# A hybrid decoder trunk: a new order of the RWKV-7 recurrence's steps, two buffers for b and the scaled k, and every level of the triangular inverse crossing array rows

## The chip, the cores and the metric

The kernel runs on one core of one Trainium2 chip. The metric is the device time of one execution in microseconds (us). Timed runs are given as the median of three. A profile is one further execution with its own time; spans in the trace are measured from its first to its last instruction.

## The reference, cut to what matters

Two layers over 256 tokens of width 1024. Layer 0 mixes with a short gated convolution, layer 1 with RWKV-7 time mixing; each is wrapped in two half-step SwiGLU networks (width 2816). All of it is float32. The part that the change touches is the time mixing of layer 1, 16 heads of 64:

```python
def step(S, inp):
    r_t, w_t, k_t, v_t, a_t, b_t = inp
    sa = jnp.einsum('bhij,bhj->bhi', S, a_t)
    S = S * w_t[:, :, None, :] + sa[..., None] * b_t[:, :, None, :] + v_t[..., None] * k_t[:, :, None, :]
    y = jnp.einsum('bhij,bhj->bhi', S, r_t)
    return S, y
...
y = wkv7_scan(rh, decay, kh, vh, -kk, kk * ah)      # kk: k scaled by k_k, normalised per head
y = group_norm(y) * ln_w + ln_b + sum(r * k * r_k) * v
out = (y * g) @ w_o
```

S is a 64x64 state per head. The kernel does not step through tokens one by one: it takes chunks of 64 tokens, in which the recurrence becomes a few 64x64 products and the inverse of a unit lower triangular 64x64 matrix.

## The kernel before, in words

The wide products (the four SwiGLU networks, the convolution's projections) run as three float32r products each (high x high, high x low, low x high); weights are loaded raw, split into a high and a low part by ScalarE (ACT) and VectorE (DVE), and multiplied on TensorE (PE). They take the span up to about 640 us and from about 910 us on.

Between lies the recurrence (`rwkv_heads`). It has eight units: unit n is a group q = n // 2 of four heads and a half t = n % 2 of the 256 tokens, that is 128 tokens or two chunks (c = 0, 1) of 64. Four heads sit as two pairs (q or p in the code) of two (e = 0, 1), and e picks the upper or lower 64 partitions. Each unit goes through four generators, which are advanced step by step:

- `front(n)`, letter F, 19 steps, F0 to F18. F0: matmul `z` (decay and gate adapters). F1: POOL `kk`, ACT tanh `sa`. F2: ACT square of `kk` into `b` (a scratch use of the buffer), DVE `am` twice. F3: matmul `cum`. F4: DVE sum `ss`, POOL power `rn`. F5: DVE `PP`, ACT exponentials `P`, `PP`. F6: POOL `rt`, DVE `kk`. F7: DVE `b`, `PP`. F8: ACT exponential `iP`, DVE `b`, `iP` (the scaled k), POOL `am`. F9, F11: PE transposes `wT`; F10, F12: ACT copies `ar`, `bk`. F13: matmuls `G`. F14: DVE predicated copy into `xfix`, then the first `pb` of the inverse. F15: DVE `br`. F16, F17: DVE `ar`, and four loads each that copy `b` and `iP` by DMA into `bkt`. F18: PE transpose `PT`, ACT `pc`, DVE `bon`.
- `inverse(n)`, letter I, 12 steps (L508 to L540). Even steps I0, I2, ... I10 are the matmuls of levels 1, 2, 4, 8, 16, 32 (eight of 64x64 stationary, 128 moving columns, 64 at level 32; a float32 matmul is two instructions in the trace, so 16). Odd steps make the next level's operands: DVE transposes `pb` out of PSUM (L512) and masks it (L514), ACT copies `xr` out of PSUM (L508); before level 32 DVE makes `p` (L519) instead. I5 and I7 also issue the loads of `hvu`, the v of chunk 0 and 1.
- `chain(n)`, letter C, 12 steps, six per chunk (`wkv_chunk`). C0: matmuls `ch<-hvu,ar`. C1: ACT copy `rc`. C2: matmuls with `tt`. C3: copies `hvu` (DVE, ACT) and `y` (ACT). C4: matmuls with `bkt` and `br`. C5: DVE `hvu` of the next chunk, DVE `y`.
- `finish(n)`, letter N, 8 steps: group norm of y on DVE, ACT and POOL, matmul `g` (N3), DVE (N4, N5), PE transposes `oT` (N6), split (N7).

A score, one string per row, gives the order in which all of this is issued. Row n (n = -2 to 7) holds front(n+2), inverse(n+1), chain(n) and finish(n-1), up to front steps that are ahead or behind. Below, "I2 of unit 3" and the like name a step and its unit. The star is a filler: half of a projection or output product, six float32r matmuls of 256 columns or three of 512 (`pj`), which need no result of the units under way. L calls `feed`, which issues the loads of filler weights (`hl_n`, 512 KB) into eight buffers, and from the 72nd filler on also the first weights of the last network (`w0h` to `w1l`); k and w load rows of vectors. The order of the score is the program order of PE, ACT and DVE, which is kept; all these loads go through SP's one queue. A last string, `end`, orders what follows row 7: the finish of unit 7, the last fillers and the first products of the last network.

In the inverse, `src` is a pair of PSUM banks, one per chunk c. A matmul of half e reads the 64 array rows of e (SBUF partitions) and writes the 64 columns `to` (PSUM partitions). At levels 1 and 32 `to` is e; at levels 2 to 16 chunk 1 writes to the other half. Buffers of the pools are released to the next writer when the last reader is done; `b` and `iP` have one buffer each.

Of the kernel before, what the change touches and what calls it, by code (L numbers as in the profile page):

```python
# [18 lines left out]
F = 2816  # L19
# [6 lines left out]
class Trunk:  # L26
# [463 lines left out]
    def wkv_inverse(self, pool, u, par, duo):  # L490

        nc = self.nc
        x1, p32 = self.xfix[par], self.p32[par]
        all4 = lambda m: m.unsqueeze(1).broadcast_to([128, 4, 64])
        by2 = lambda z: z.rearrange("p (c q) m -> p c q m", c=2)
        src = duo.rearrange("p c (q i m) -> p c q i m", q=2, i=2)

        def ready(l):  # L500

            old = by2(x1[:, :, 1]) if l == 1 else src[:, :, :, 1]
            xr = pool.tile([128, 4, 2, 64], F32, name=f"xr{par}", bufs=1) if l > 1 else x1

            def rest():
                if l > 1:
                    n = 2 if l < 32 else 1
                    nc.scalar.copy(xr.rearrange("p (c q) i m -> p c q i m", c=2)[:, :, :, 0:n], src[:, :, :, 0:n])  # L508

            if l < 32:  # L510
                pb = pool.tile([128, 4, 64], F32, name=f"pb{par}", bufs=1)
                nc.vector.transpose(by2(pb), old)  # L512
                rest()
                nc.vector.tensor_tensor(pb, pb, all4(self.lev[l]), ALU.mult)  # L514
            else:
                pb = p32
                for e in range(2):
                    lo, hi = slice(64 * e, 64 * e + 32), slice(64 * e + 32, 64 * e + 64)
                    nc.vector.transpose(by2(pb)[hi, :, :, 0:32], old[lo, :, :, 32:64])  # L519
                rest()  # L520
            return pb, xr

        pb, xr = ready(1)
        yield
        for l in (1, 2, 4, 8, 16, 32):
            n = 2 if l < 32 else 1
            for q in range(2):
                for c in range(2):
                    for e in range(2):

                        to = e ^ (c if 1 < l < 32 else 0)
                        re, out = slice(64 * e, 64 * e + 64), slice(64 * to, 64 * to + 64)
                        i = 2 * c + q
                        self.mm(src[out, c, q, 0:n], pb[re, i], xr[re, i, 0:n])
            yield
            if l < 32:
                pb, xr = ready(2 * l)
            else:
                u["tt"] = pool.tile([128, 2, 2, 64], F32, name="tt", bufs=2)
                nc.scalar.copy(u["tt"], src[:, :, :, 0])  # L540
            yield
# [288 lines left out]
    def rwkv_heads(self, pool, prm, krv, lora, gT, g2, rows, row_tile, P, loaded, follow,  # L830
# [5 lines left out]
        T2 = lambda name, b=1: pool.tile([128, 256], F32, name=name, bufs=b)  # L836
# [5 lines left out]
        def front(n):  # L842
# [3 lines left out]
            u = dict(bon=s4("bon", 4), hvu=[])  # L846
            us.append(u)
            k, r = (krv[q, i][:, t] for i in "kr")
            P, iP, PP, kk, b, am, rt = (T2(i) for i in ("P", "iP", "PP", "kk", "b", "am", "rt"))

            sa = pool.tile([128, 2, 256], F32, name="sa")
            z = self.tr_bank("z").rearrange("p (i n) -> p i n", i=2)
# [45 lines left out]
            for pair, own in (((PP, rt), True), ((b, iP), False)):  # L898
# [6 lines left out]
                for j in range(2):  # L905
                    if own:
                        for e in range(2):
                            re = slice(64 * e, 64 * e + 64)
# [143 lines left out]
        def filler():  # L1052
# [15 lines left out]

        score = (
            'FFF',  # L1070
            '***LFFFFF****FLFFFF***FLF****LFFF***FLFF****FL',
            'I*FFILFFFII**FFLFII**FFILIFF*LkFIIF**FFLIIFFF**L',
            'I*FCFIFL*CFFICCIL*F*FICFFICFICLCFILCIFFICFF*FLIICCFFF**L',
            'I*FCFIFL**CNFFICNCINL**F*FICFFICFNICLNCFINLkCIFFINCFF**NFLIICCFFF**L',
            'I*FCFIFL*CNFFICNCINL**F*FICFFICFNICLNCFINLCIFFINCFF*NFLIICCFFF**Lw',
            'I*FCFIFL**CNFFICNCINL**F*FICFFICFNICLNCFINLkCIFFINCFF**NFLIICCFFF**L',
            'IFCFIFL*CNFFICNCINL*FFICFFICFNICLNCFINLCIFFINCFF*NFLIICCFFF*Lw',
            'I**FCFIFCLNFFICNICN**FLFF**ICICNFIFCFLCNINF**LCIFICFF**NFNLIICC**L',
            'ICI*CLICNNICN**LICICNILCCNINL*CIICN*NLIICC*Lw',
            'CCL*CNNC*NLC*C*LNCCN*NLCC*NNL*CC*L',  # L1080
        )
        fronts = (step for n in range(8) for step in front(n))
        feed()
        for _ in score[0]:
            next(fronts)
        with self.tc.manual_schedule(engines={mybir.EngineType.Activation, mybir.EngineType.DVE}):
            for n, order in zip(range(-2, 8), score[1:]):
                steps = dict(F=fronts, C=chain(n) if n >= 0 else None, N=finish(n - 1) if n >= 1 else None,
                             I=us[n + 1]["inv"] if -1 <= n < 7 else None)
# [16 lines left out]

        post = lambda: posts.popleft()()
        last = finish(7)
        end = 'NN*N**LLL**L*L*L*LLL**PNLNP01NNN2ooooP3P4567'
        for i in end:  # L1110
            if i == "N":
                next(last)
# [90 lines left out]
```

## Time and profile before

| | us |
|---|---|
| median of 3 runs | 1098.09 |
| lowest, highest | 1096.61, 1101.34 |
| the profiled execution | 1098.65 |
| its span in the trace | 1096.9 |

| engine | busy us | share of the span | instructions |
|---|---|---|---|
| PE (matmul) | 1063.9 | 97% | 6480 |
| DVE | 687.4 | 63% | 980 |
| ACT | 529.2 | 48% | 781 |
| POOL | 99.7 | 9% | 179 |

Busy time of an engine is the union of its instructions' durations. PE's matmuls overlap one another, so a busy PE need not be a PE at its peak; where small matmuls run, the distance from one start to the next tells more. The idle time before an instruction is shown in brackets with what ended it. In the windows view each row is one stretch: its length, then busy time (and number of instructions) of PE, PEld (weight loads), DVE, ACT and POOL in this order, then the granted TensorE clock as a share of full speed (1.00 is 2.4 GHz, half is 1.2 GHz), the DMA engines' busy share and the GB/s moved.

### The profile page before, as it was taken

Reading aid. Unit: us, or ns where it says so; the run is one execution under the profiler, and the core shown is the slowest. Engines: PE = TensorE matmul, PEld = TensorE weight load, DVE = VectorE, ACT = ScalarE, POOL = GpSimd, SP = SyncE. Lnnn points to the kernel's source line nnn. Section 1 sums busy time; section 2 is a strip of 40 time slices with the busy share of each in tenths; the row PEclk is TensorE's granted clock in tenths of the full one; section 3 lists DMA queues with packets and bytes.
Section 4 is the critical chain, followed back from the end, with each engine's and each line's share of the span. In section 5 each row is a group of like instructions: output and inputs, shape, how many; then the busy total and the mean of one; then the engine's idle time right before and its main releaser. Section 6 shows DMA issues by size and latency. Waiting matters only on the chain.

```text
span 1096.9 us, 16693 instructions
## 1 busy us (share of the span) xinstructions
PE 1063.9 (97%) x6480; PEld 875.9 (80%) x6480; DVE 687.4 (63%) x980; ACT 529.2 (48%) x781; POOL 99.7 (9%) x179
## 2 busy tenths in 40 slices
PE   7999999999999999999999999998998989999997
PEld 5888888788878888887888888987877768888886
DVE  5666554786666654567665546657889866555534
ACT  7555443655565554356544433434544426444342
POOL 6000000000320000000000001212423210000000
PEclk9999999999999999999999999999999999999999
DMA  8998877698699987679998854774553846666541
GB/s 287 314 294 273 292 244 258 210 360 269 202 302 345 284 285 261 210 260 309 320 295 296 295 191 138 275 231 147 163 160 119 269 133 191 190 191 208 179 170 39
DMA packets 178167, 259.39 MB, mean 236 GB/s; under 512 B 24238, under 2 KB 142758, under 8 KB 178088
## 3 DMA queue, kind: packets, MB, share of 16 engines
q1 hardware_dynamic: 178088, 258.32, 71.4%
q8 instruction: 51, 0.84, 0.3%
q14 instruction: 28, 0.23, 0.1%
HBM read 216.34 MB, written 38.80 MB: 233 GB/s over the span
## 4 chain that ended last, share of the span: by engine, by line
PE 68%; issue 18%; DVE 6%; DMA 3%; ACT 2%; SPq 2%; POOL 0%; POOLq 0%; ACTq 0%; DVEq 0%
PE gu L113 10%; PE gu L114 9%; PE gu L112 9%; PE acc L113 5%; PE acc L114 5%; PE acc L112 5%; PE pair L113 2%; PE pair L114 2%; PE pair L112 2%; PE ci L113 2%; PE ci L114 2%; PE ci L112 2%; SPq L50 2%; PE pj L112 2%; PE aT L351 1%
## 5 line engine op out<-in xcount | busy, mean ns | idle before, releaser
L107 DVE TENSOR_TENSOR lo_gu<-raw_gu,hi_gu 128x2048 fp32r<-128x2048 f32 (+2 forms) x92 | 198.5, 2160 | 109.6 <-ACT hi_gu L106 106.0
L113 PE MATMUL gu<-lo_gu,xh 128*128 128x512 f32 x640 | 252.9, 395 | 2.9 <-DVE lo_gu L107 2.9
L114 PE MATMUL gu<-hi_gu,xl 128*128 128x512 f32 x640 | 252.8, 395 | 0.0
L112 PE MATMUL gu<-hi_gu,xh 128*128 128x512 f32 x640 | 250.4, 394 | 1.0 <-ACT xh L178 1.0
L106 ACT CAST hi_gu<-raw_gu 128x2048 fp32r<-128x2048 f32 (+2 forms) x92 | 164.9, 1796 | 33.7 <-PE gu L114 11.8
L107 DVE TENSOR_TENSOR lo_o<-raw_o,hi_o 128x2048 fp32r<-128x2048 f32 x48 | 109.2, 2291 | 112.4 <-ACT hi_o L106 111.1
L113 PEld LDWEIGHTS gu<-lo_gu,xh 128*128 128x128 f32 x640 | 120.5, 188 | 28.5 <-DVE lo_gu L107 4.9
L106 ACT CAST hi_o<-raw_o 128x2048 fp32r<-128x2048 f32 x48 | 90.7, 1909 | 103.2 <-PE acc L114 68.5
L112 PEld LDWEIGHTS gu<-hi_gu,xh 128*128 128x128 f32 x640 | 120.4, 188 | 24.8 <-ACT xh L178 1.4
L114 PEld LDWEIGHTS gu<-hi_gu,xl 128*128 128x128 f32 x640 | 120.5, 188 | 23.6 <-DVE xl L180 0.4
L113 PE MATMUL acc<-lo_o,ah 128*128 128x512 f32 (+1 forms) x316 | 122.4, 387 | 1.4 <-DVE lo_o L107 1.4
L114 PE MATMUL acc<-hi_o,al 128*128 128x512 f32 (+1 forms) x316 | 122.4, 387 | 0.0
L112 PE MATMUL acc<-hi_o,ah 128*128 128x512 f32 (+1 forms) x316 | 117.4, 388 | 0.0
L345 ACT ACTIVATE s<-gu,rs 128x256 f32<-128x256 f32 x80 | 38.0, 475 | 97.2 <-PE gu L114 97.2
L150 POOL TENSOR_TENSOR rs<-ms,fixed 128x1 f32<-128x1 f32 x14 | 8.9, 638 | 817.9 <-DVE ms L148 817.7
L113 PEld LDWEIGHTS acc<-lo_o,ah 128*128 128x128 f32 x316 | 59.4, 188 | 13.6 <-DVE lo_o L107 1.8
L112 PEld LDWEIGHTS acc<-hi_o,ah 128*128 128x128 f32 x316 | 59.4, 188 | 11.9
L114 PEld LDWEIGHTS acc<-hi_o,al 128*128 128x128 f32 x316 | 59.4, 188 | 11.8
L117 ACT CAST ah<-aT 128x512 fp32r<-128x512 f32 x44 | 25.8, 586 | 82.2 <-PE aT L351 82.1
L349 DVE SCALAR_TENSOR_TENSOR a<-gu,rs,s 128x256 f32<-128x256 f32 x80 | 38.1, 481 | 35.3 <-ACT s L345 35.3
L602 ACT CAST hl_p<-hl_p 128x512 fp32r<-128x512 f32 x72 | 44.3, 624 | 28.3 <-DMA hl_p<-in_rwkv_w_rkv_dram 19.2
L603 DVE TENSOR_TENSOR hl_p<-hl_p 128x512 fp32r<-128x512 f32 x72 | 48.3, 686 | 4.0 <-ACT hl_p L602 3.7
(270 smaller groups left out, 1674.6 us busy)
## 6 DMA issues: line engine op xcount, KB each, us to landing
raw_gu<-in_ffn_w_gu_dram SPq DMA_DIRECT2D x164, 512.0 KB, 5.6
raw_o<-in_ffn_w_d_dram SPq DMA_DIRECT2D x44, 1024.0 KB, 5.9
parts<-hl_p SPq DMA_DIRECT2D x72, 512.0 KB, 7.0
hl_n<-parts SPq DMA_DIRECT2D x52, 512.0 KB, 4.6
hl_p<-in_rwkv_w_rkv_dram SPq DMA_DIRECT2D x48, 256.0 KB, 7.3
raw_ci<-in_conv_w_in_dram SPq DMA_DIRECT2D x14, 512.0 KB, 7.7
raw_ci<-in_conv_w_in_dram SPq DMA_DIRECT2D x4, 1024.0 KB, 8.1
raw_o<-in_conv_w_out_dram SPq DMA_DIRECT2D x4, 1024.0 KB, 8.8
```

Source lines behind the costliest of these rows:

```text
L50: return self.tc.keep_in_program_order(self.nc.sync.dma_start(dst, src))
L106: nc.scalar.copy(hi[:, ks], raw[:, ks])
L107: nc.vector.tensor_tensor(lo[:, ks], raw[:, ks], hi[:, ks].bitcast(F32), ALU.subtract)
L112: keep(mm(out, xh, wh, start=start, stop=False))
L113: keep(mm(out, xh, wl, start=False, stop=False))
L114: keep(mm(out, xl, wh, start=False, stop=stop))
L117: keep(self.nc.scalar.copy(hi, src))
L345: act = nc.scalar.activation(s, ps[t][:, 0:256], AF.Silu, scale=rstd[t])
L349: nc.vector.scalar_tensor_tensor(a, ps[t][:, 256:512], rstd[t], s, ALU.mult, ALU.mult)
L351: nc.tensor.transpose(out=pt[:, j, t * 128:t * 128 + 128], in_=a[:, j * 128:(j + 1) * 128], identity=self.ident)
L602: nc.scalar.copy(hi, lo)
L603: nc.vector.tensor_tensor(lo.bitcast(F32R), lo, hi.bitcast(F32), ALU.subtract)
```

## The change

Three edits. The crossing of chunk 1 to the other half of the columns is done at all six levels (the slice `out` is `e ^ c` always). `b` and `iP` get two buffers each; the other front tiles keep one. The ten rows of the score after the first, and the string `end`, are written anew with the same letters in all (96 fillers, 60 feeds, 149 F after the first three, 96 I, 96 C, 56 N); where a row's count changes, steps pass to a neighbour row. Fillers by row, from -2 to 7: before 21, 10, 7, 10, 8, 10, 4, 12, 6, 8; after 20, 11, 8, 9, 8, 8, 6, 11, 7, 8.

```diff
@@ wkv_inverse
-                        to = e ^ (c if 1 < l < 32 else 0)
-                        re, out = slice(64 * e, 64 * e + 64), slice(64 * to, 64 * to + 64)
+                        re, out = slice(64 * e, 64 * e + 64), slice(64 * (e ^ c), 64 * (e ^ c) + 64)
                         i = 2 * c + q
                         self.mm(src[out, c, q, 0:n], pb[re, i], xr[re, i, 0:n])
@@ front
-            P, iP, PP, kk, b, am, rt = (T2(i) for i in ("P", "iP", "PP", "kk", "b", "am", "rt"))
+            P, PP, kk, am, rt = (T2(i) for i in ("P", "PP", "kk", "am", "rt"))
+            iP, b = (T2(i, 2) for i in ("iP", "b"))
@@ score (rows -2 to 7)
-            '***LFFFFF****FLFFFF***FLF****LFFF***FLFF****FL',
-            'I*FFILFFFII**FFLFII**FFILIFF*LkFIIF**FFLIIFFF**L',
-            'I*FCFIFL*CFFICCIL*F*FICFFICFICLCFILCIFFICFF*FLIICCFFF**L',
-            'I*FCFIFL**CNFFICNCINL**F*FICFFICFNICLNCFINLkCIFFINCFF**NFLIICCFFF**L',
-            'I*FCFIFL*CNFFICNCINL**F*FICFFICFNICLNCFINLCIFFINCFF*NFLIICCFFF**Lw',
-            'I*FCFIFL**CNFFICNCINL**F*FICFFICFNICLNCFINLkCIFFINCFF**NFLIICCFFF**L',
-            'IFCFIFL*CNFFICNCINL*FFICFFICFNICLNCFINLCIFFINCFF*NFLIICCFFF*Lw',
-            'I**FCFIFCLNFFICNICN**FLFF**ICICNFIFCFLCNINF**LCIFICFF**NFNLIICC**L',
-            'ICI*CLICNNICN**LICICNILCCNINL*CIICN*NLIICC*Lw',
-            'CCL*CNNC*NLC*C*LNCCN*NLCC*NNL*CC*L',
+            '**F*FFFL***FFLFF*FF***FL**F*FLFF****LFF*FF*L*',
+            'FIFIF*F*IFL**IFF*FL*IILF*FIILFF*kFIIF**FLFIIFFLF*',
+            'I*FCFIFL*CFICLF*I*CFFICFFIL*CFICICFILCFI*CFFF*FLIILCCF*',
+            'FFFI*FFCLC*NFI*FCNCILIN*F*FICFFICFNICLNCFINLkCIFINCFF*F**NFLIICCFFF*L',
+            'FI*CLFIFFCNFI*CNCIN**LF*FICFFIFCNICLNCILNFCIFINFCFF**NFLIICCFFF*Lw',
+            '*IFCFI*CNFLNFFICCIN*L**FFICFFICICLFNCNLINFkCIFFINC*FF*F*NLICICFFFL',
+            '*IFFIC*LCFIFNCNC*INF*L*FFICFFICFILFNCNCNLCIIFIFCNFFF*ICCLNLwI',
+            'FFF*I*FCFIFC*LNFICNIF*CN**FLFFICICNFIFCFLNINCI*LCFFICFLF**NI*ICN*CL',
+            'FICI*CNNIC*LLICN*I*CICNILCCNINL*CIINCN*L*IICCLw',
+            'CNCL*NCC*NL*CC*LNNCNC*LCC*NNL*CC*L',
@@ end
-        end = 'NN*N**LLL**L*L*L*LLL**PNLNP01NNN2ooooP3P4567'
+        end = 'NN*N**LLL***L*L*LLLL*N*PLNPN01NN2ooooP3P4567'
```

## Rows read from the trace of the kernel before

**Rows 1.** The profile page: span, and busy time of TensorE.
```profile
span 1096.9 us, 16693 instructions
...
PE 1063.9 (97%) x6480; PEld 875.9 (80%) x6480; DVE 687.4 (63%) x980; ACT 529.2 (48%) x781; POOL 99.7 (9%) x179
```

**Rows 2.** Windows view, one row per unit, from level 1 of units 0 to 7.
```profile
723.72:741.49 17.77, 15.80 (x205) 13.48 (x205) 12.03 (x28) 7.96 (x19) 4.07 (x5) 1.00 0.70 225
741.49:761.89 20.40, 17.58 (x271) 14.44 (x271) 14.57 (x39) 9.89 (x28) 4.46 (x7) 1.00 0.50 154
761.89:782.44 20.55, 20.00 (x287) 16.85 (x286) 17.28 (x46) 10.21 (x29) 6.61 (x8) 1.00 0.53 161
782.44:802.58 20.14, 19.09 (x283) 15.85 (x282) 18.15 (x48) 10.29 (x29) 6.85 (x10) 1.00 0.45 133
802.58:823.57 20.99, 20.13 (x287) 16.88 (x287) 17.78 (x46) 10.69 (x30) 6.64 (x8) 1.00 0.62 177
823.57:842.61 19.04, 16.62 (x259) 13.02 (x258) 17.58 (x46) 9.29 (x28) 6.92 (x10) 1.00 0.28 79
842.61:863.62 21.01, 20.63 (x266) 15.34 (x265) 18.92 (x48) 9.56 (x28) 5.54 (x7) 1.00 0.75 234
863.62:880.45 16.83, 14.32 (x205) 10.05 (x205) 13.61 (x37) 5.59 (x16) 2.40 (x3) 1.00 0.88 291
880.45:896.50 16.05, 15.63 (x118) 11.16 (x119) 9.31 (x24) 3.66 (x12) 2.34 (x4) 0.89 0.15 48
```

**Rows 3.** Timeline of TensorE: start, length, instruction, [idle before it, what ended it].
```profile
782.44 1.09 PE L54 MATMUL pair<-xfix,pb 64*64 64x128 f32 x16
...
790.90 0.45 PE L54 MATMUL ch<-hvu,br 64*64 64x64 f32 x8
...
792.93 0.67 PE L54 MATMUL pair<-xr,pb 64*64 64x128 f32 x16
...
798.61 0.68 PE L54 MATMUL pair<-xr,p 64*64 64x64 f32 x16 [0.65 <-ACT xr L508]
```

**Rows 4.** Timeline of ScalarE: the two long waits of F2.
```profile
725.50 0.42 ACT L860 ACTIVATE b<-kk 128x256 f32<-128x256 f32 x1 [3.89 <-DMA bkt<-b]
...
744.06 0.42 ACT L860 ACTIVATE b<-kk 128x256 f32<-128x256 f32 x1 [3.29 <-DMA bkt<-b]
```

**Rows 5.** Timeline of TensorE: the waits that follow those two.
```profile
727.60 0.34 PE L54 MATMUL pair<-xr,pb 64*64 64x128 f32 x4 [1.45 <-ACT xr L508]
...
746.16 0.34 PE L54 MATMUL pair<-xr,pb 64*64 64x128 f32 x4 [0.72 <-ACT xr L508]
...
747.39 0.27 PE L54 MATMUL ch<-rc,tt 64*64 64x64 f32 x2 [0.57 <-ACT rc L559]
```

**Rows 6.** Timeline of SP's queue: weight loads, and the hvu loads behind them.
```profile
866.41 0.51 SPq L50 DMA_DIRECT2D hl_n<-parts  x1
...
872.55 4.36 SPq L50 DMA_DIRECT2D hvu<-pv  x4
```

**Rows 7.** Timeline of TensorE in row 7 of the score.
```profile
880.45 1.21 PE L54 MATMUL ch<-hvu,ar 128*64 128x64 f32 x16 [2.22 <-DMA hvu<-pv]
...
884.07 0.50 PE L112 MATMUL pj<-hl_n,oh 128*128 128x512 f32 x1
...
888.86 0.69 PE L54 MATMUL ch<-hvu,ar 128*64 128x64 f32 x16
...
890.74 0.50 PE L112 MATMUL pj<-hl_n,oh 128*128 128x512 f32 x1
```

**Rows 8.** Windows view of the stretch behind that wait (clock 0.63).
```profile
880.45:885.00 4.55, 4.55 (x34) 3.06 (x34) 0.28 (x1) 1.08 (x4) 0.00 (x0) 0.63 0.51 166
```

**Rows 9.** Timeline of VectorE at the start of unit 3's level 1 turnaround.
```profile
783.58 0.45 DVE L512 STREAM_TRANSPOSE pb<-pair 128x256 f32<-128x256 f32 x1 [0.40 <-PE pair L54]
...
784.91 0.42 DVE L873 TENSOR_TENSOR PP<-cum,sa 128x256 f32<-128x256 f32 x1 [0.42 <-PE cum L54]
```

**Rows 10.** Timeline of TensorE in the end string, unit 7's transposes.
```profile
902.40 0.33 PE L57 MATMUL oT<-fixed,y 128*128 128x128 f32 x1 [0.51 <-DVE y L993]
```

## The prediction

> **What bounds the kernel now.** The page comes first: TensorE is busy for 1063.9 of 1096.9 us [rows 1], so time can come only from the 33 us in which it idles or from matmuls that take longer than they need. The windows, unit by unit, say where the idle time lies. Before 640 us TensorE is dense; in the nine stretches from 723.72 to 896.50 us, which are rows -1 to 7 of the score, it idles (length less PE busy) 1.97, 2.82, 0.55, 1.05, 0.86, 2.42, 0.38, 2.51 and 0.42 us, together 13.0 us [rows 2]. The same rows give the second limit. VectorE idles only 3.27, 1.99, 3.21, 1.46 and 2.09 us in rows 1 to 5 (lengths 19.04 to 21.01), and part of this is the pause between its 46 to 48 instructions. So the full rows are bound by two engines at once: TensorE first, VectorE one to three us behind. The timelines then name the waits. Six are long enough to count alone: 1.45, 0.72 and 0.57 us [rows 5], 2.22 us [rows 7], 0.65 us at level 32 [rows 3] (such a wait stands in five units: four of 0.65, one of 0.34), 0.51 us in the end string [rows 10].
>
> **The crossing.** At level 1 the sixteen instructions take 1.09 us, at a crossed level of the same shape 0.67 us [rows 3]: the crossed four start together, the uncrossed in twos. That is 0.42 us less for level 1 in each of eight units. Level 32, uncrossed, takes 0.68 us; a crossed level with 64 columns isn't in the trace. Its bounds: nothing saved (0.68), or as many starts as the eight instructions of `ch<-hvu,br`, four pairs of 64 columns in 0.45 us [rows 3], so 0.23 saved; below nothing I see no reason, since the same four squares of the array are used at levels 2 to 16. I take 0.23, because the level with 128 columns did gain by four starts. Sum: 8 x (0.42 + 0.23) = 5.2 us, bounds 3.4 and 5.2. No instruction is added; six crossings bring chunk 1 back to its half as four did.
>
> The Trainium skill, TensorEngine Tiling (Array Packing), section Restrictions and Gotchas, says that different row tiles cannot access the same PSUM bank simultaneously. In this kernel e = 0 and e = 1 are two row tiles that write one chunk's bank, in different partitions. By that rule the two would take turns, crossed or not, and the sum of this part would be 0; the row with 0.67 us for the crossed level speaks against it.
>
> **Two buffers for b and iP.** F2 writes its square into `b` while the previous unit's `bkt` loads still read it: ScalarE waits 3.89 and 3.29 us for that DMA [rows 4]. Behind the square stand F4's sum on VectorE, then the level's transposes (VectorE takes its instructions in the written order), then ScalarE's `xr`, and TensorE waits 1.45 us in row -1, 0.72 + 0.57 us in row 0 [rows 5]. With two buffers the last reader of the buffer is a whole unit back (some 20 us), so both waits go: 2.74 us. What is late next is `cum` and the turnaround itself, which have two fillers beside them in the new rows. Later units lack the wait, since their F2 comes after the loads. Nothing is added on a queue. Bounds: 0 (another link holds level 2 as long) to 2.74; I take 2.7.
>
> **The loads of unit 7's v.** The 2.22 us wait is for `hvu` [rows 7]. Counting what each L issues: before, the fourth weight batch since row 5 (two `hl_n`, four pieces of the last network's weights, 2 MB) is issued in row 6 just ahead of I5 of unit 7, so the `hvu` loads stand behind it in SP's queue: the batch is issued from 866.41 us, `hvu` from 872.55 us, with 4.36 us for four issues [rows 6], while the DMA engines are 0.88 busy at 291 GB/s in this row [rows 2]. At that rate 2 MB are 7 us. In the new row 6 the two L stand together two fillers earlier and find no free buffer, so the batch moves to the L after I6, behind chunk 0's `hvu`. Chunk 0's loads then come at least the wait earlier: 2.22 us. Chunk 1's stand behind the batch, but are read only in the middle of row 7. The batch itself serves the end string.
>
> Right after that wait the granted clock is 0.63 over 4.55 us [rows 8], a stretch at the half level. C0, filler, C2 up to the next filler take 3.62 us there (880.45 to 884.07), and 1.88 us for the same steps of chunk 1 (888.86 to 890.74) [rows 7]: 1.74 us lost. Without the wait I expect no drop: 1.7 us. Bounds for the whole part: 0 (the loads stay late) to 3.9.
>
> **The end string.** N3 to N5 come before the first products of the last network, so N6 finds y finished: 0.5 us [rows 10], with 0 as the other bound.
>
> **The order.** Idle time left in rows 2 is 13.0 - 2.7 - 2.2 = 8.1 us: the bounds of what order alone can give are 8.1 and, since waits can also be made, some way below nothing. What I see in it: fillers go from rows that are full (row 3: 10 to 8, row 5: 12 to 11) to rows where TensorE waits (row 4: 4 to 6, where it idles 2.42 us; row -1; row 6), which costs nothing where it fills waits. F15 (`br`, a product of the kind that takes 0.42 us in rows 9) goes behind I9, so `p` for level 32 is made earlier, and the fillers before F18 are split, against the 0.65 us. In row 1 `cum` goes ahead of level 1, so VectorE has `PP` to do in place of its two waits of 0.40 and 0.42 us [rows 9]. Against it: in row 3 I6 follows I4 with only C4 and F11 between, N3 having moved behind; in row 4 I7 stands behind the four VectorE products of N4 and N5; F1 to F3 of unit 3 have one filler in place of two. I take 2.5 us won, about a third of 8.1, because the level 32 waits alone are 2.9 (four of 0.65, one of 0.34), and 2.5 us lost again: 0.5 in the places just named, and 2.0 because in rows 2, 4 and 5, where VectorE idles least, the crossing's 0.65 us each only moves TensorE into waiting.
>
> **Sum.** 5.2 + 2.7 + 2.2 + 1.7 + 0.5 + 2.5 - 2.5 = 12.3 us. All of it lies in the chain, since TensorE is dense again from the first products of the last network on. The profiled execution took 1098.65 us (span 1096.9), 0.6 above the median of the runs; 1098.65 - 12.3 = 1086.3, and from the median 1085.8. I forecast 1086.
>
> **Rivals.**
> 1. VectorE becomes the bound of rows 1 to 6. For it: idle times of 1.5 to 3.3 us there [rows 2]; against it: these are still more than the 0.65 us per row that the crossing takes. The crossing then pays only in two of the eight units and order gives nothing: 12.3 - 2.5 - 6 x 0.65 + 2.0 = 7.9, so 1090.7. Chance 0.25.
> 2. `hvu` of unit 7 is still late, behind the batch of row 5 that is issued at that row's end, and the clock falls again: 12.3 - 3.9 = 8.4, so 1090. For it: DMA busy at 0.88 in that row. Chance 0.12.
> 3. Slower: the turnaround of a level runs out of cover. Between two levels stand `pb` (a transpose of 0.45 us [rows 9] and a masking product) and `xr`; a unit has six such turns, so 48. If the new order puts one VectorE product of 0.42 us [rows 9] ahead of each and no filler beside it, 48 x 0.42 = 20 us come in, less 12.3: 1106. It decides from 12.3 / 48 = 0.26 us per turnaround on. For it: VectorE's density; against it: the new rows keep most groups of F and I as they were. Chance 0.09.
> 4. The crossing does not do what it says, because the two row tiles of one bank take turns: 12.3 - 5.2 = 7.1, so 1091.5. Levels 2 to 16 speak against it. Chance 0.03. This is where the Trainium skill's rule above would lead.
> 5. The new order makes as many waits as it takes away while one of the other parts fails: some 3.5 us won, 1095. Chance 0.10.
>
> **How the numbers follow.** The forecast has 0.41, its own range 1082 to 1089. About 0.5% (5.5 us) is what a measurement of this kernel can tell from no change; the bound is 1092.6. Faster: 0.40 of the forecast, 0.21 of rival 1, 0.10 of 2, 0.02 of 4, 0.01 of 5: 0.74. Slower, past 1103.6: rival 3, 0.08. Same: the rest, 0.18. The range is 1080 to 1096: below, order gives 6 of the 8.1 us and loses nothing; above, rivals 1, 2 and 5 are in; rival 3 is left out.
>
> **What would show it.** Level 1's sixteen matmuls in 0.67 us and level 32's in 0.45. No wait of `b` for `bkt` on ScalarE, and level 2 of unit 0 without its 1.45 us. C0 of unit 7 without a wait for `hvu`, and a granted clock of 1.00 in that stretch. TensorE idle under 9 us from level 1 of unit 0 to the end of row 7. Wrong would be: matmul starts of level 1 still in twos; VectorE idle under 1 us in rows 1 to 5 with TensorE idle as before; a new wait of over 1 us at `pair<-xr,pb` in rows 3 or 4.

## The result and the profile after

| | before | after |
|---|---|---|
| median, us | 1097.35 (1095.72 to 1101.34, 4 runs) | 1086.56 (1086.32 to 1088.63, 4 runs) |
| ratio, 95% interval | | 0.9898 [0.9879, 0.9917] |
| profiled execution, its span, us | 1098.65, 1096.9 | 1088.63, 1086.9 |

The time lies 0.6 us from the forecast, inside the range and 10.8 us under the time before. First the page of the changed kernel, beside [rows 1]: the work is the same (6480 matmul records), TensorE is busy 3.8 us less and the span is 10.0 us shorter.

```profile
span 1086.9 us, 16688 instructions
...
PE 1060.1 (98%) x6480; PEld 872.9 (80%) x6480; DVE 686.5 (63%) x980; ACT 528.8 (49%) x781; POOL 100.1 (9%) x179
```

Where it lies is told by one window over the whole recurrence, from its first matmul `z` to the first `gu` product of the last network (the products that `end` issues lie inside). Windows view; before, then after (columns as in [rows 2]):

```profile
703.97:914.61 210.64, 197.08 (x2434) 159.46 (x2432) 160.10 (x408) 95.71 (x262) 53.41 (x71) 0.99 0.56 171
```

```profile
705.65:904.60 198.95, 190.98 (x2434) 154.06 (x2432) 159.36 (x408) 95.50 (x262) 53.94 (x71) 1.00 0.59 181
```

The recurrence is 11.69 us shorter: 5.59 us of TensorE's idle time (13.56 to 7.97) and 6.10 us of its busy time. What follows takes 182.3 us in both. What comes ahead is 1.68 us longer in this execution of after (705.65 instead of 703.97): its granted clock is 0.91 over the first 20 us, where before has 1.00 and which the change does not touch, and its other three runs lie some 2 us lower. The length of the recurrence is used below for the experiments, since it leaves such things out. Windows view of after, rows -1 to 7, which answers to [rows 2]:

```profile
725.00:740.30 15.30, 15.30 (x209) 13.42 (x209) 10.32 (x24) 7.47 (x19) 3.71 (x5) 1.00 0.84 284
740.30:759.00 18.70, 17.88 (x279) 14.85 (x278) 15.24 (x40) 9.82 (x28) 4.46 (x7) 1.00 0.65 200
759.00:778.37 19.37, 18.89 (x281) 15.56 (x281) 17.79 (x46) 10.54 (x30) 6.52 (x8) 1.00 0.52 151
778.37:797.48 19.11, 18.80 (x287) 15.65 (x287) 17.83 (x48) 10.22 (x30) 7.12 (x10) 1.00 0.44 133
797.48:816.38 18.90, 18.12 (x276) 14.86 (x275) 17.17 (x44) 10.04 (x30) 6.66 (x8) 1.00 0.70 182
816.38:836.87 20.49, 17.57 (x272) 13.91 (x271) 17.93 (x47) 9.80 (x29) 7.13 (x10) 1.00 0.37 112
836.87:856.18 19.31, 19.18 (x256) 13.77 (x255) 18.49 (x47) 9.44 (x27) 5.76 (x7) 1.00 0.76 223
856.18:872.17 15.99, 14.23 (x209) 9.91 (x208) 12.92 (x37) 5.63 (x17) 2.28 (x3) 1.00 0.95 304
872.17:886.28 14.11, 14.11 (x118) 10.09 (x119) 10.02 (x26) 3.59 (x12) 2.38 (x4) 1.00 0.18 65
```

Length less PE busy is 0, 0.82, 0.48, 0.31, 0.78, 2.92, 0.13, 1.76 and 0 us, together 7.2 where 13.0 stood. Two rows keep a hole: row 4 (816.38), which had 2.42, and row 6 (856.18). The granted clock is 1.00 in every row. Timeline of TensorE of after: a last level (32) and the first level behind it, and the waits that are left:

```profile
793.40 0.41 PE L57 MATMUL PT<-fixed,P 128*128 128x128 f32 x2 [0.28 <-DVE br L930]
793.74 0.46 PE L54 MATMUL pair<-xr,p 64*64 64x64 f32 x16
...
797.48 0.67 PE L54 MATMUL pair<-xfix,pb 64*64 64x128 f32 x16
...
823.35 0.41 PE L57 MATMUL wT<-fixed,PP 128*128 128x128 f32 x2 [0.99 <-DVE PP L881]
...
832.90 0.41 PE L57 MATMUL PT<-fixed,P 128*128 128x128 f32 x2 [1.30 <-DVE br L930]
...
872.17 0.69 PE L54 MATMUL ch<-hvu,ar 128*64 128x64 f32 x16 [1.62 <-issue]
...
890.04 0.50 PE L114 MATMUL pair<-w0h,xl 128*128 128x512 f32 x1 [0.77 <-DVE xl L180]
```

### The profile page after: what moved, and what is told of

It reads as the page before. It is cut to its first block, busy times and chain, and to the rows that moved or that the text cites. A ratio compares the mean times of both kernels' runs of the same rounds, so it can differ in the third digit from the quotient of the medians.

```text
span 1086.9 us, 16688 instructions
## 1 busy us (share of the span) xinstructions
PE 1060.1 (98%) x6480; PEld 872.9 (80%) x6480; DVE 686.5 (63%) x980; ACT 528.8 (49%) x781; POOL 100.1 (9%) x179
## 4 chain that ended last, share of the span: by engine, by line
PE 73%; issue 18%; DVE 5%; ACT 1%; DMA 1%; SPq 1%; POOL 0%; POOLq 0%; DVEq 0%; ACTq 0%
PE gu L113 10%; PE gu L114 10%; PE gu L112 10%; PE acc L113 5%; PE acc L114 5%; PE acc L112 5%; PE pj L112 2%; PE pair L114 2%; PE pair L113 2%; PE pair L112 2%; PE ci L113 2%; PE ci L114 2%; PE ci L112 2%; PE pj L113 2%; PE pj L114 2%
## 5 line engine op out<-in xcount | busy, mean ns | idle before, releaser
L150 POOL TENSOR_TENSOR rs<-ms,fixed 128x1 f32<-128x1 f32 x14 | 11.2, 798 | 819.7 <-DVE ms L148 819.5
```

The costliest lines, as they stand in the source:

```text
L150: self.last_rs = nc.gpsimd.tensor_tensor(rs, ms[:, 1:2], self.nhalf[:, 0:1], ALU.pow)
```

## The experiments

Each was timed in turn with the kernel before on one chip. Before has its own column, since the groups ran on different chips, which differ by over 1 us: compare medians down the column only with that in mind. The clock is the mean granted clock of the runs (before: 0.9971, 23 runs, in the first group). The last column, the median of each run's time multiplied by its own clock, is an estimate of the time at full clock, in which all of the time is taken to follow the clock; for before it is some 1094 to 1095. The clock of a run is known to three digits (half a us), and where a part of the time does not follow the clock the estimate is too low: a straight line through the 12 runs of the crossing alone reaches 1094.1 us at clock 1.00, one through the 23 runs of before beside it 1095.2. The profile is that of one of the runs. For the crossing alone it is the longest of its 12 (1105.92 us, clock 0.986), for the kernel with levels 1 and 32 twice the shortest (1094.96 us, clock 0.999), so the lengths of these two recurrences differ by far more than their medians.

| kernel | median us (runs) | before, same chip | ratio [95%] | recurrence in the profile, us | clock | at full clock |
|---|---|---|---|---|---|---|
| before + crossing | 1100.78 (12) | 1098.19 | 1.0024 [1.0009, 1.0038] | 217.86 | 0.9914 | 1090.7 |
| before + buffers | 1096.16 (12) | 1098.19 | 0.9986 [0.9974, 0.9999] | 210.46 | 0.9972 | 1093.3 |
| before + order | 1094.30 (5) | 1098.19 | 0.9965 [0.9951, 0.9978] | 206.09 | 0.9978 | 1091.4 |
| after without crossing | 1090.31 (5) | 1098.19 | 0.9933 [0.9919, 0.9947] | 202.72 | 0.9988 | 1089.2 |
| after without buffers | 1091.22 (6) | 1096.77 | 0.9953 [0.9937, 0.9970] | 202.27 | 0.9968 | 1087.7 |
| before + early `hvu` loads | 1094.62 (12) | 1096.77 | 0.9979 [0.9967, 0.9991] | 209.26 | 0.9971 | 1091.3 |
| before + crossing + buffers | 1096.01 (12) | 1097.98 | 0.9975 [0.9957, 0.9993] | 206.91 | 0.9934 | 1088.6 |
| before + crossing, levels 1 and 32 twice | 1096.94 (12) | 1097.98 | 0.9992 [0.9978, 1.0006] | 206.60 | 0.9978 | 1094.5 |
| after | 1086.56 (4) | 1097.35 | 0.9898 [0.9879, 0.9917] | 198.95 | 0.9988 | 1085.8 |

**The crossing alone, in the old order.**

```diff
-                        to = e ^ (c if 1 < l < 32 else 0)
-                        re, out = slice(64 * e, 64 * e + 64), slice(64 * to, 64 * to + 64)
+                        re, out = slice(64 * e, 64 * e + 64), slice(64 * (e ^ c), 64 * (e ^ c) + 64)
```

> The kernel before with the crossing at levels 1 and 32 alone. Theory (the crossing is worth what its matmuls lose): level 1 goes from 1.09 to 0.67 us, level 32 from 0.68 to 0.45, 0.65 us in each of eight units, so 5.2 us less, ratio 0.9953. Rival (VectorE bounds rows 1 to 6): the same shorter levels, but TensorE waits as much longer in those rows, and 1.3 us are left, ratio 0.9988. If level 32 does not start in fours, 3.4 us.

It is slower, which was not foreseen: 2.6 us by the medians. In this profile, the longest of the 12 runs, the recurrence is 7.2 us longer than in before, with less work in it. Windows view of this kernel, the recurrence and three short stretches:

```profile
704.02:921.88 217.86, 202.41 (x2433) 163.17 (x2432) 159.22 (x408) 95.64 (x262) 53.38 (x71) 0.94 0.55 165
...
729.00:733.00 4.00, 4.00 (x33) 3.48 (x32) 2.37 (x6) 2.53 (x7) 0.72 (x1) 0.57 1.02 381
749.50:753.50 4.00, 3.97 (x28) 3.69 (x28) 2.62 (x6) 1.63 (x5) 1.75 (x5) 0.57 0.75 246
804.00:808.00 4.00, 4.00 (x22) 3.63 (x16) 2.93 (x11) 0.90 (x2) 0.00 (x1) 0.57 0.18 74
```

The clock is 0.57 in these stretches, most of each at the lower level, and as low at three more places of the recurrence; before has one such stretch [rows 8], which is also the last of these six. What TensorE did just ahead of the three shown is in its timeline:

```profile
728.14 0.67 PE L54 MATMUL pair<-xr,pb 64*64 64x128 f32 x16 [2.37 <-ACT xr L508]
...
748.29 0.67 PE L54 MATMUL pair<-xr,pb 64*64 64x128 f32 x16 [1.73 <-ACT xr L508]
...
802.58 0.46 PE L54 MATMUL pair<-xr,p 64*64 64x64 f32 x16 [0.65 <-ACT xr L508]
803.30 0.45 PE L574 MATMUL ch<-hvu,bkt 128*64 128x64 f32 x8 [0.26 <-ACT y L570]
```

The waits that were 1.45 and 0.72 us [rows 5] are 2.37 and 1.73. Some 0.4 us of each increase is the time that level 1 saves: `xr` still comes when ScalarE is through with its own wait for the DMA, so there the saved time turns into idle time. The rest is that wait itself, which in this execution was 4.39 and 3.88 us where before had 3.89 and 3.29 [rows 4]. At level 32 the saving is lost too in five of the eight units: it takes 0.46 instead of 0.68 us, but right behind it comes a new wait of 0.26 us for ScalarE's `y`, where before has none, and the next matmuls start 0.72 us after level 32 in both. Elsewhere the saving of level 1 stays: row 3, at clock 1.00, takes 20.15 us (808.13 to 828.28), and 20.58 in the next kernel, in which these levels take as long as uncrossed.

So the crossing alone does save time, but less than its 5.2 us: at full clock this kernel would stand at 1090.7 to 1094.1 us, between 1 and 4 us under before by the same two estimates. The fallen clock takes more than that back. It falls behind the two long waits and, as at 804 us, behind the short ones of level 32 (0.65 and 0.26 us), where before has 0.65 us alone and kept 1.00 in its profile.

**Is it the clock?** The same kernel with the eight matmuls of levels 1 and 32 issued twice (the second time the same values into the same place), so that each level takes as long as uncrossed (1.10 and 0.69 us in its timeline): more work, and the saved time is not idle time.

```diff
-            for q in range(2):
+            for q in (0, 1) * (2 if l in (1, 32) else 1):
```

> The crossing alone, with the matmuls of levels 1 and 32 issued twice (the second writes the same values), so that these levels take about as long as uncrossed. It has 128 matmul instructions more at level 1 and 128 more at level 32 than the crossing alone and no wait less. Theory (the clock is what the crossing alone lost): the mean granted clock comes back to about 0.997, the time to that of the kernel before or less, ratio 0.998 to 1.000, so faster than the crossing alone (1.0024) with more work. Rival (the crossed matmuls themselves cost something, such as a change of the array's rows and columns): it costs twice as often, ratio 1.005 or above.

With 256 more matmul records the median of 12 runs is 3.8 us lower than with the crossing alone, on another chip; the intervals of the two ratios do not touch. Between the two profiles, the longest run of the one and the shortest of the other, the recurrence is 11.3 us shorter. Windows view:

```profile
704.28:910.88 206.60, 195.88 (x2689) 158.79 (x2688) 159.24 (x408) 95.71 (x262) 53.42 (x71) 1.00 0.58 174
```

The clock is 1.00, and 0.9978 in the mean of the 12 runs where the crossing alone has 0.9914. Matmuls that compute nothing new make the kernel faster, so it was the shorter work, by way of the clock, that did the harm, and not the crossed matmuls, of which there are more here. At full clock this kernel is not faster than before (1094.5).

**The buffers alone.**

```diff
-            P, iP, PP, kk, b, am, rt = (T2(i) for i in ("P", "iP", "PP", "kk", "b", "am", "rt"))
+            P, PP, kk, am, rt = (T2(i) for i in ("P", "PP", "kk", "am", "rt"))
+            iP, b = (T2(i, 2) for i in ("iP", "b"))
```

> The kernel before with two buffers for b and iP alone. Theory: ScalarE's waits of 3.89 and 3.29 us for the bkt loads go, and with them TensorE's 1.45, 0.72 and 0.57 us: 2.7 us less, ratio 0.9975. Rival: another link of the chain (cum, P, the next xr) holds level 2 in rows -1 and 0 as long, and nothing is won, ratio 1.000.

Level 2 of units 0 and 1, the two places of [rows 5] (timeline of TensorE):

```profile
728.90 0.67 PE L54 MATMUL pair<-xr,pb 64*64 64x128 f32 x16 [0.31 <-ACT xr L508]
...
748.92 0.67 PE L54 MATMUL pair<-xr,pb 64*64 64x128 f32 x16 [0.31 <-ACT xr L508]
```

In this profile rows -1 and 0 take 16.59 and 18.80 us, 2.78 less than in [rows 2], against 2.7 in the forecast. The recurrence as a whole is only 0.2 us shorter in this one execution: its clock falls at two places (797.9 us, behind a wait of 0.64 us at level 32, and 879.9 us) where before's does so once, and C0 of unit 7 waits 3.08 us for `hvu` where it waited 2.22 [rows 7], so that a part of what was won is waited for there. By the medians 2.0 us are left.

**Crossing and buffers, old order.** Both edits on the kernel before.

> The kernel before with the crossing and the two buffers, old order. Theory (the crossing alone lost because TensorE then rests longer in the old order's waits and its granted clock falls to half; the buffers take the two longest of these waits away): the mean clock is nearer to that of the kernel before (0.997) than to that of the crossing alone (0.991), and the time is 3 to 5 us less than before, ratio 0.9955 to 0.997. Rival (the crossing is worth nothing in the old order, whatever the clock): as the buffers alone, ratio 0.9986 or above.

The clock comes only part of the way back, 0.9934 after 0.9914 (0.9971 before), and the ratio 0.9975 misses the range that was expected: the two waits of the buffers are not the only places where the crossing costs clock. In this profile it falls at three, behind the waits of level 32 in rows 0 and 4 and at C0 of unit 7, which waits 2.24 us for `hvu`. The place in row 0 (windows view, timeline of TensorE):

```profile
756.00:760.00 4.00, 4.00 (x24) 3.58 (x26) 2.30 (x8) 0.90 (x2) 0.51 (x1) 0.57 0.24 94
```

```profile
754.22 0.46 PE L54 MATMUL pair<-xr,p 64*64 64x64 f32 x16 [0.65 <-ACT xr L508]
```

The median is 4.8 us under that of the crossing alone, on two chips. By the two ratios the crossing is worth 1.2 us beside the buffers (0.9986 to 0.9975), and 3.5 to 4.7 at full clock.

**The order alone.** The score and the string `end` of after in the kernel before.

> The kernel before with the new score and end string alone, no crossing, one buffer each. Theory (the parts add up): the whole change is 11.2 us by its ratio, less 5.2 and 2.7, so 3.3 us less, ratio 0.997. Rival A (the order carries most, the other parts only fit it): 8 us or more, ratio under 0.993. Rival B (the order only works with the shorter levels and free buffers): nothing or slower, since F2 and F4 now stand earlier beside the loads and one buffer makes them wait.

3.9 us under before by the medians, some 3.2 at full clock (1094.6 on this chip). The old buffers hold the new order up: in row 0 ScalarE waits 3.13 us for `bkt`, TensorE 1.28 and 0.57 us behind it, the clock falls, and the row takes 22.48 us, 18.70 in after.

**After without the crossing.**

```diff
-                        re, out = slice(64 * e, 64 * e + 64), slice(64 * (e ^ c), 64 * (e ^ c) + 64)
+                        to = e ^ (c if 1 < l < 32 else 0)
+                        re, out = slice(64 * e, 64 * e + 64), slice(64 * to, 64 * to + 64)
```

> The changed kernel with levels 1 and 32 uncrossed again. Theory: 5.2 us slower than the changed kernel, so 6.0 less than before, ratio 0.9945. Rival (VectorE bounds the rows): only 1 to 2 us slower than the changed kernel, ratio about 0.991.

```profile
703.44:906.16 202.72, 195.54 (x2434) 158.82 (x2433) 159.71 (x408) 95.65 (x262) 54.07 (x71) 1.00 0.58 177
```

In the new order the crossing is worth 3.77 us in the profile (202.72 to 198.95, windows view, both at clock 1.00) and 3.75 by the medians, on two chips. This lies between the 5.2 us of the theory and the 1 to 2 of its rival. Row by row, from -1 to 5: 0.66, 0.47, 0.42, 0.51, 0.36, 0.30 and 0.63 us. Row -1, where VectorE is busy for only two thirds, keeps all of it; the full rows keep half to all.

**After without the buffers.**

```diff
-            P, PP, kk, am, rt = (T2(i) for i in ("P", "PP", "kk", "am", "rt"))
-            iP, b = (T2(i, 2) for i in ("iP", "b"))
+            P, iP, PP, kk, b, am, rt = (T2(i) for i in ("P", "iP", "PP", "kk", "b", "am", "rt"))
```

> The changed kernel with one buffer each for b and iP. Theory (the parts add up): 2.7 us slower than the changed kernel, some 8.4 less than before, ratio 0.992. Rival A (the parts only work together): F2 waits for the bkt loads again, TensorE thins out in rows -1 and 0, the granted clock falls to its half level there as it did with the crossing alone, and 5 us or more are lost, ratio over 0.9945. Rival B: the new order lets F2 come late enough, nothing is lost, ratio 0.990.

Timelines of ScalarE and TensorE in row 0, the only one where a wait comes back:

```profile
741.69 0.42 ACT L859 ACTIVATE b<-kk 128x256 f32<-128x256 f32 x1 [3.58 <-DMA bkt<-b]
...
743.79 0.67 PE L54 MATMUL pair<-xr,pb 64*64 64x128 f32 x16 [2.15 <-ACT xr L508]
```

The chain is that of [rows 4, 5]: `b` waits for the DMA that reads its old content, `xr` comes late, TensorE waits 2.15 us and 0.57 more further on. The row takes 21.91 us instead of 18.70, and the recurrence 3.3 us more. By the medians it is 4.7 us, on two chips; at full clock 1.9. The ratio, 0.9953, misses the theory and lies where rival A put it; in this profile the clock stays at 1.00 in row 0, but its mean over the six runs is 0.9968 after 0.9988, so the fall of the clock is seen in the runs and not placed. Row -1 has the same length as in after: there the new order alone had taken TensorE's wait away.

**The loads of `hvu` early, in the old order.**

```diff
-                if i in (6, 8):
-                    c = i // 2 - 3
+                if i in (2, 4):
+                    c = i // 2 - 1
```

> The kernel before with the hvu loads issued at I1 and I3 in place of I5 and I7. Theory: C0 of unit 7 no longer waits 2.22 us for the load, and TensorE's clock falls less often behind it: 2 to 4 us less than before, ratio 0.9965 to 0.998. Rival A: C0 then waits for VectorE's y of the chunk before (its chunk bank has one buffer), and under 1 us is won. Rival B: the loads land as late, behind the weight batch of row 5: no change.

```profile
880.25 0.36 PE L54 MATMUL ch<-hvu,ar 128*64 128x64 f32 x5 [0.35 <-PE pj L114]
```

With the loads issued ahead of the weight batch, C0 of unit 7 (timeline of TensorE) waits 0.35 us in place of 2.22 [rows 7]: the queue was the cause in the kernel before. By the medians the edit is worth 2.2 us, near the 1.87 us of the wait; the 1.7 us of the clock did not come with it here. In this profile's windows the clock is 1.00 behind C0, but it falls to the lower level at 840 us, the end of row 4, behind a wait of 0.65 us at level 32 (838.00), where before has the same wait and kept 1.00:

```profile
840.00:844.00 4.00, 4.00 (x22) 3.51 (x22) 2.38 (x9) 0.90 (x2) 0.38 (x1) 0.50 0.06 15
...
880.00:891.00 11.00, 10.34 (x97) 7.03 (x99) 7.68 (x20) 2.79 (x10) 2.28 (x3) 1.00 0.40 144
```

**What is left in after.** Four kernels tried the holes that its rows 4 and 6 and its end string show. The first puts the last filler of row 6 between the last chain step of unit 6 and C0 of unit 7:

```diff
-            'FICI*CNNIC*LLICN*I*CICNILCCNINL*CIINCN*L*IICCLw',
+            'FICI*CNNIC*LLICN*I*CICNILCCNINL*CIINCN*LIICC*Lw',
```

> The changed kernel with the last filler of row 6 moved from ahead of I10 to behind C11. In the changed kernel C0 of unit 7 waits 1.62 us; by the times of its row this is for VectorE's y (done at 872.06, C0 starts at 872.17), not for a load. Theory: the moved filler covers 0.7 us or more of this wait, 0.5 to 1 us less than the changed kernel, ratio about 0.989. Rival: the wait is for a load and only moves: the same time as the changed kernel, and a wait of over 0.9 us left.

```profile
866.83 0.38 PE L54 MATMUL pair<-xr,p 64*64 64x64 f32 x9 [0.26 <-ACT xr L508]
867.55 0.34 PE L574 MATMUL ch<-hvu,bkt 128*64 128x64 f32 x4 [0.26 <-ACT y L570]
...
869.62 0.39 PE L54 MATMUL ch<-hvu,ar 128*64 128x64 f32 x6 [0.35 <-PE pj L114]
```

The wait goes from 1.62 to 0.35 us (timeline of TensorE), and two of 0.26 come in where the filler stood. The recurrence is 0.44 us shorter; the median, 1086.33 (1086.08 to 1086.64, 5 runs; ratio 0.9907 [0.9893, 0.9922]), can't be told from that of after.

The second adds two fillers to row 4 on top of that edit, taken from row -2, with `r` of the next group looked up at F6:

```diff
-            '**F*FFFL***FFLFF*FF***FL**F*FLFF****LFF*FF*L*',
+            '**F*FFFL***FFLFF*FF**FL**F*FLFF***LFF*FF*L*',
...
-            '*IFFIC*LCFIFNCNC*INF*L*FFICFFICFILFNCNCNLCIIFIFCNFFF*ICCLNLwI',
+            '*IFFIC*LCFIFNCNC*INF*L**FFICFFICFILFNCNCNLCIIFIFCNFF*F*ICCLNLwI',
```

> As x7_row6, and two fillers moved from row -2, where TensorE does not wait, to row 4, where it waits 0.99 us ahead of F9 and 1.30 us ahead of F18 in the changed kernel; r is looked up at F6 so that its projection may end later. Theory: both waits go, 1.4 us less (two fillers of 0.72 us), 2 to 2.5 us less than the changed kernel, ratio 0.9875. Rival (VectorE's queue bounds row 4): fillers there only delay what VectorE waits for, the waits move on, and nothing is won over x7_row6.

Windows view of rows -2, 0 and 4 of this kernel:

```profile
704.16:722.08 17.92, 17.92 (x163) 17.01 (x162) 9.41 (x22) 8.12 (x19) 4.16 (x5) 1.00 0.63 188
...
737.39:756.77 19.38, 18.31 (x279) 14.83 (x278) 15.26 (x40) 9.88 (x28) 4.48 (x7) 1.00 0.64 191
...
815.33:835.97 20.64, 19.18 (x284) 15.37 (x283) 17.63 (x47) 10.19 (x30) 7.23 (x10) 1.00 0.44 132
```

Row 4 takes both fillers for 0.15 us (20.49 in after, with 1.6 us less TensorE work), so its hole is filled. Row -2 is 1.42 us shorter (19.34 in the kernel above). But row 0 is 0.7 us longer than in after, row 1 (19.90) 0.5, row 3 (19.49) 0.6, for reasons that were not followed up. 1087.30 us (1086.18 to 1088.75, 5 runs; 0.9914 [0.9899, 0.9928]): nothing won.

The third has the first's edit and the old fillers, and moves two steps of row 4 (I4 ahead of F9, N3 ahead of F13):

```diff
-            '*IFFIC*LCFIFNCNC*INF*L*FFICFFICFILFNCNCNLCIIFIFCNFFF*ICCLNLwI',
+            '*IFFIC*LCFIFNCNC*INF*L*FIFCFFICFILNFCNCNLCIIFIFCNFFF*ICCLNLwI',
```

> As x7_row6, with two steps swapped in row 4: I4 ahead of F9, and N3 ahead of F13. Theory (VectorE's queue bounds row 4 of the changed kernel, and in it stand two waits of its own, 0.64 us for I4, which stands behind F9 on TensorE, and 0.72 us for N3's matmul, which stands behind F13): both go, 1.0 to 1.4 us less than x7_row6 (1086.3), so about 1085.1. Rival (the order of TensorE's steps there only shifts the waits to ScalarE's copies for F9 and F13): within 0.3 us of x7_row6.

```profile
821.77 0.41 PE L57 MATMUL wT<-fixed,PP 128*128 128x128 f32 x2 [0.31 <-DVE PP L881]
...
824.60 0.67 PE L54 MATMUL pair<-xr,pb 64*64 64x128 f32 x16 [0.85 <-ACT xr L508]
...
831.07 0.41 PE L57 MATMUL PT<-fixed,P 128*128 128x128 f32 x2 [1.00 <-DVE br L930]
```

The wait of `wT` shrinks from 0.99 to 0.31 us and that of `PT` from 1.30 to 1.00, but I6 now waits 0.85 instead of 0.26 (timeline of TensorE). 1086.43 us (1085.44 to 1088.32, 6 runs; 0.9896 [0.9874, 0.9918]): the waits were for the most part moved, not removed (2.56 us of idle time in the row after 2.92). Two of the three are for VectorE's results, the third for ScalarE's `xr`.

The last takes the first's and the third's edits and an end string with N3 to N5 spread:

```diff
-        end = 'NN*N**LLL***L*L*LLLL*N*PLNPN01NN2ooooP3P4567'
+        end = 'NN*N**LLL***L*L*LLLL**PNLPNN01NN2ooooP3P4567'
```

> As x10_row4b, and in the end string the finish's matmul N3 stands between the two posts in place of ahead of them, N4 and N5 behind them, so that VectorE makes xl before the y products. In the changed kernel the first products of the last network wait 0.77 us for xl there. Theory: this wait goes and no other takes its place, 0.5 to 0.8 us less than x10_row4b (1086.4), so about 1085.8, the fastest of all. Rival: N6 then waits for y as it did for 0.51 us in the kernel before, and 0.3 us or less is won, which the runs cannot tell.

```profile
889.42 0.44 PE L57 MATMUL oT<-fixed,y 128*128 128x128 f32 x2 [0.51 <-DVE y L993]
```

The 0.77 us wait for `xl` in after is gone and the 0.51 us of [rows 10] is back (timeline of TensorE). 1085.66 us (1085.34 to 1086.49, 6 runs; 0.9881 [0.9861, 0.9901]) is the lowest median of all, but its interval covers that of after, and it is not told apart from it.

## Why the prediction was right, point by point

**The crossing: right in size, but with a condition that the forecast did not state.** Level 1 takes 0.67 us and level 32 0.46 in after (0.67 and 0.45 forecast). Net of the 2.0 us that the full rows were to give back, 3.2 us were expected, and 3.75 were measured; rows 2, 4 and 5, which were to give all of it back, keep 0.51, 0.30 and 0.63. What failed is a step that was not there: that the saving is one in any order. In the old order the crossing made the kernel 2.6 us slower by the medians, beside the buffers 1.2 us faster by the ratios, and only with the new order 3.75. Rival 4 is out: were the row tiles of one bank to take turns, level 1 could not have gone from 1.09 to 0.67 us; four of its instructions start together at 778.37 in after, where at 782.44 in before two do.

**The buffers: right.** 2.78 us against 2.7 in the old order's two rows. In the new order the same edit was worth 3.3 us in the profile, nearly all of it in row 0. No `b` waits for `bkt` any more. The medians of the old order show 2.0 us, since a part came back as a longer wait for `hvu`.

**The loads of unit 7's v: the cause right, the size not.** In after, SP's timeline has `hvu` of chunk 0 ahead of the weights, at 860.21 us instead of 872.55 [rows 6]:

```profile
859.70 0.47 SPq L50 DMA_DIRECT2D w1l<-parts  x1
860.21 1.27 SPq L50 DMA_DIRECT2D hvu<-pv  x2
861.58 0.54 SPq L50 DMA_DIRECT2D hl_n<-parts  x1
```

Still C0 of unit 7 waits 1.62 us, to 872.17 (timeline above). What ends just ahead of it is on VectorE's timeline:

```profile
870.39 0.68 DVE L1018 TENSOR_TENSOR x<-x,pj 128x512 f32<-128x512 f32 x1
870.98 0.58 DVE L581 TENSOR_TENSOR hvu<-ch,pc 64x128 f32<-64x128 f32 x2
871.48 0.58 DVE L584 TENSOR_TENSOR y<-ch,y 64x128 f32<-64x128 f32 x2
```

The sum of a filler's product stands in front of the chain's last two products, which end at 872.06 us. The profile names no releaser for C0; that it waited for these is read from the times and from the kernel with the filler moved, where 0.35 us is left. So 2.22 was mis-sized: 0.6 us came of it. The question "what is late next" was put for the buffers and not here. The 1.7 us of the clock did come: 1.00 in the stretch behind C0, where before had 0.63 [rows 8]. Row 7 is 1.94 us shorter.

**The end string: wrong, and small.** The 0.51 us wait went, a 0.77 us wait for `xl` came: -0.26 instead of +0.5.

**The order: 2.5 won and 2.5 lost were expected; the reason failed in one row.** The fillers that row 4 got were to fill its waits. It takes 20.49 us after 19.04, with 2.92 idle after 2.42: its waits are for VectorE's `PP` and `br`, and the places where the fillers stand are others. This is the place that rival 1 named, VectorE as bound, and the second and third kernels of the last group bear that out for row 4 alone, which takes 1.6 us more TensorE work at nearly the same length. What the forecast set against level 32's waits held: none of the eight units waits there in after (793.74 is one of them), where six had 0.25 to 0.65 us in before. At full clock the order is worth some 3 us on top of the other two edits (1088.6 to 1085.8, an estimate), but 8.5 by the two ratios (0.9975 to 0.9898); the rest goes with the clock, since the loss that the crossing brings in the old order (0.9934) is gone in the new one (0.9988).

**The clock: a term of the whole, priced at one place.** The forecast had 1.7 us for one stretch. By the mean clocks, before loses 0.0029 x 1098 = 3.2 us (2.9 to 3.8 on the other chips) and after 0.0012 x 1087 = 1.3 (estimates, time that follows the clock), so 1.6 to 2.5 us of the gain are the clock's, close to the 1.7. What the forecast missed is that parts of the change, taken alone, move this term by 6 us (from 3.2 to 9.5 with the crossing), so they do not add up: alone they win -2.6, +2.0 and +3.9 us by the medians, 3.3 together, where the whole wins 10.8.

The Trainium skill, TensorE: Matmul & The Clock Gate, section A second HAM failure mode: psum-queue depth-cycling, tells of a kernel whose TensorE idles briefly but often between groups of matmuls, and whose clock swings between its two levels for that. The trace of the crossing alone agrees in that the clock falls between its levels behind waits among small groups of matmuls (0.65 and 0.26 us, then 0.57 of full clock); that cycling PSUM banks cause the waits, as in the page's kernel, no run here shows. By that passage a loss of clock could have stood among the rivals for the crossing; the sum would have come out the same, since in the new order the clock stays at 1.00.

**The sum: in part luck.** The loads and the end string fell short by 2.4 us (1.6 and 0.8). The rows gave more: of the 11.69 us of the recurrence, 9.4 are left without the `hvu` wait, the end string and row 7, and for the crossing, the buffers and the order together 7.9 were forecast. The two cancel for the most part.

**What stays open.** The old order with crossing and buffers runs at 0.9934, with the buffers alone at 0.9972. In the profiles of four old-order kernels (crossing, buffers, both, early `hvu` loads) the clock falls behind a wait at level 32, which the new order doesn't have; but before has that wait at 1.00, so a wait there does not always bring a fall, and no run took away these waits alone. Whether a cheaper VectorE step in row 4 would pay wasn't tried.

## What to carry to other kernels

A faster matmul group in front of a fixed wait saves nothing at that place, and the kernel can lose more than the group saves elsewhere when the granted clock falls behind the longer wait; give it cover (fillers, an earlier producer) in the same change, and read the granted clock of both traces, and of all runs, before the times. When a stall's cause is taken away, name what is late next at that very place: here 1.62 of 2.22 us stayed. Parts that interact through the clock have to be tried on the finished order, by taking one out, rather than on the old one.

## What the runs showed of the hardware that was not expected

**Less work, slower.** The crossing alone takes 5.1 us of matmul time away (eight times 0.42 and 0.22) and the kernel takes 2.6 us more (ratio 1.0024 [1.0009, 1.0038]); with empty work in the same places the time falls by 3.8.

**The spread of the runs is largely the clock's.** The times of the 23 runs of before on one chip go with their granted clocks (correlation -0.85; on the other three chips -0.67, -0.90 and -0.89).

**VectorE beside POOL.** A VectorE product of two 128x256 operands takes 0.42 us alone (at most 0.48 in the 117 between 690 and 930 us of after that no POOL product of this size overlaps), and mostly 0.8 to 1.0 us where it overlaps one by over half a us. Timelines of VectorE and of POOL, after:

```profile
819.73 0.82 DVE L974 SCALAR_TENSOR_TENSOR y<-s,y 128x256 f32<-128x256 f32 x1
...
822.04 0.83 DVE L880 SCALAR_TENSOR_TENSOR b<-sa,kk 128x256 f32<-128x256 f32 x1
...
872.56 0.42 DVE L974 SCALAR_TENSOR_TENSOR y<-s,y 128x256 f32<-128x256 f32 x1
```

```profile
819.54 0.73 POOL L877 TENSOR_TENSOR rt<-pr,P 128x256 f32<-128x256 f32 x1 [0.64 <-ACT P L874]
...
821.98 0.61 POOL L981 TENSOR_TENSOR bv<-pv,bon 128x256 f32<-128x256 f32 x1 [1.70 <-DVE s L978]
```

The first two run beside `rt` and `bv`, the third, of the first's line, beside nothing. Both slow ones stand ahead of the `PP` for which `wT` waits in row 4.
